# A two-layer trunk on one core: the first norm's order and c's row, the low parts of the out stage, and the place of the tiles in memory

## The chip, the core and the metric

The kernel runs on one core of one Trainium2 chip. The core has five engines that run side by side, each with its own instruction stream: TensorE (PE in the profile; its weight loads are listed as PEld), VectorE (DVE), ScalarE (ACT), GpSimd (POOL) and SyncE (SP), which issues most of the DMA transfers. Engines wait for one another by semaphores. Operands lie in SBUF (128 partitions), matmul results in PSUM.

The metric is the device time of one execution in microseconds. The time of a kernel is the median of its runs. Times inside the kernel come from one execution that the hardware profiler recorded.

## What is computed

A trunk of two layers over 512 frames of 1024 channels, in fp32. Cut to what matters here (first the silu of the conditioning vector c, from which each layer's six rows of shift, scale and gate come):

```python
def rms_norm(x, g):
    return x * lax.rsqrt(jnp.mean(x * x, axis=-1, keepdims=True) + 1e-6) * g

c_act = jax.nn.silu(c)                               # c: 1024 values
for l in range(2):
    sh1, sc1, gt1, sh2, sc2, gt2 = jnp.split(c_act @ ada_w[l] + ada_b[l], 6)
    h = rms_norm(x, norm1_g[l]) * (1 + sc1) + sh1
    p = h @ w_in[l]                                  # and v_down for the second layer
    ...                                              # token shift, split of p
    y_a = rwkv7_time_mix(...)                        # chunks of 64 frames, 8 heads
    y_b = multiscale_pool(...)
    mixed = br_gate[0] * (y_a @ proj_a[l]) + br_gate[1] * (y_b @ proj_b[l])
    x = x + gt1 * (mixed @ w_out[l])
    h2 = rms_norm(x, norm2_g[l]) * (1 + sc2) + sh2
    gate, up = jnp.split(h2 @ w_gu[l], 2, axis=-1)
    x = x + gt2 * ((silu(gate) * up) @ w_down[l])
return rms_norm(x, final_g)
```

## The kernel before

x is kept with channels on the partitions: eight tiles of 128 channels x 512 frames. A norm therefore needs sums over partitions, which TensorE makes.

**Products in three parts.** For accuracy every fp32 operand of the large products is split into a high part (rounded to the type fp32r) and a low part (what is left). A `block` is three matmuls: high weights by high data, high weights by low data, low weights by high data (`hh,whi`, `hl,whi`, `hh,wlo`). All matmuls go through one helper, so all of them have line L221. `weights` (from L179) makes the two parts of a weight tile of 128x1024 that SP has fetched (`raw`): ScalarE casts the high part (L195), and the low part is made in one of two ways. Either VectorE subtracts (L201), or, while `self.by_dma` is set, ScalarE writes the negative of the raw tile (L198) and GpSimd issues a DMA that adds the weight from memory once more onto it, the rounding being left over since the destination was written as fp32r (L199):

```python
if self.by_dma and (self.by_dma is True or self.count % self.by_dma):
    nc.scalar.activation(lo, raw, AF.Copy, scale=-1.0)
    nc.gpsimd.dma_start(lo, src, accum_op=ALU.add)
else:
    self.on(nc.vector, "tensor_tensor")(lo, raw, hi.bitcast(F32), ALU.subtract)
```

Of the tiles that the profile names, `hh` and `hl` are the parts of the normed x, `yah` and `yal` those of the time-mixing result, `mh` and `ml` those of the merged branches (`mixed`), `f`, `fh`, `fl` those of the channel mixer's inner values, `th`, `tl`, `f13h`, `f13l` those of products of 256 columns in the mixer (function `seven`), in which seven products take the place of eight.

**The head** (`head`, from L294) is the first norm. SP issues c, given out to all 128 partitions in the transfer (L299), the eight pieces of x (L302), two tables of constants (L304, L305), the first two rows of ada_w (`raw`, L255) and then pieces of w_in (`wr`, L322). ScalarE takes the Silu of c on all partitions (`cact`, L310) and the squares of the pieces of x (`ssum` for the first, `sq` for the others, L398 and L401; two buffers), VectorE sums the squares (L402). In `rstd` TensorE then multiplies the sum with a column of 1/1024 (`m<-mean,ssum`), ScalarE takes the root (`r`, L413), VectorE the reciprocal (L414), and multiplies it into four diagonal matrices (`dg`, L417); one product of them with ones (`m<-dg,ones`) gives the factor of each frame on all partitions. VectorE then makes `nt` (x times that factor, L354), ScalarE `nh` (scale and shift, L356), and w_in's first products, in plain fp32 (`acc<-nh,wr`), begin. The shift and scale (`mods`) come from VectorE's passes over rows of ada_w times cact (`modulation`, L264, two instructions each, a custom operation and a read-out), and `gsc` (L289) joins the scale with the norm's gain. `soon` (L391) is a tiny activation that loads a function table of ScalarE ahead of its use.

**The order of the work.** A scheduler orders each engine's instructions by the dependencies and the order in which the code issues them. Where the code sets `pinned` (for TensorE) or `exact` (for ScalarE and VectorE; `on` consults it), the order of the program is kept.

**The out stage** stands at the end of the mixer of each layer, behind the last chunks of the time mixing. `side` (L512) multiplies the pooled branch with proj_b and the gate (`hh`, `hl` in L533 are its results here, kept in buffers of those names). `mixer` (from L1131) then loops over eight output tiles m: twelve matmuls of proj_a with `yah`, `yal`; the gate `g` comes by DMA, `g` times the product (L1150), plus the other branch (L1151), then the split into `mh` on ScalarE (L245) and `ml` on VectorE (L246). In the loop the weights of proj_a (four tiles) and the first two of w_out are prepared. `by_dma` is set in the stages before and is switched off behind this loop, ahead of the products with w_out. `yn` (L1010) and `yal` (L1029) belong to the last step of the time mixing.

**Memory.** Tiles are laid out in pools that are opened and closed from both ends of SBUF. By the tables of the built program the places of the tiles within 512 bytes are: whi, wlo, hh, hl and raw at 96; f, fh, fl, th, tl, f13h, f13l and the other factors at 480; xi, wr, mh, ml at 160; two small pools at 64. No matmul operand of the three-part products lies at 0.

Of the kernel before, what the change touches and what calls it, by code (L numbers as in the profile page):

```python
# [17 lines left out]
DRAM = bass.MemoryType.DRAM  # L18

P = 128  # L20
D = 1024
S = 512
L = 2
# [50 lines left out]
FINAL = (6, 3)  # L74

WHOLE = 3

EARLY = ((2, 5, 5, 4), (3, 6, 6, 6))

# [42 lines left out]
class Trunk:  # L122
    def __init__(self, ctx, tc, a, out):
        self.ctx, self.tc, self.nc, self.a, self.out = ctx, tc, tc.nc, a, out
        self.pinned, self.last, self.by_dma = False, None, False
        self.third, self.turn, self.ahead, self.on_way, self.land = None, 0, 1, [], []
        self.count, self.fetched = 0, []
        self.hf, self.exact, self.later, self.keep = None, False, [], 0
        self.after = None
        nc = self.nc  # L130
        pool = lambda **k: ctx.enter_context(self.pool(**k))
        self.const = pool(name="const", bufs=1)
        self.wraw = pool(name="wraw", bufs=3)
        self.whl = pool(name="whl", bufs=2)
        self.hp = pool(name="hp", bufs=1)
        self.psum = pool(name="psum", bufs=4, space=PSUM)
        self.dram = pool(name="dram", bufs=1, space=DRAM)
        self.cst = self.const.tile([P, N_CST], F32, name="cst")
        self.cols = self.const.tile([P, N_COLS], F32, name="cols")
        self.ones = self.const.tile([P, P], F32, name="ones")  # L140
        self.mean = self.const.tile([P, 1], F32, name="mean")
        self.eps = self.const.tile([P, 2], F32, name="eps")
        self.mods = [self.const.tile([P, 48], F32, name=f"mods{l}") for l in range(L)]
        self.gsc = [self.const.tile([P, 16], F32, name=f"gsc{l}") for l in range(L)]
        self.omm = [self.const.tile([P, 15], F32, name=f"omm{l}") for l in range(L)]
        self.omka = [self.const.tile([P, 4], F32, name=f"omka{l}") for l in range(L)]
        self.xs = [self.dram.tile([P, S], F32, name=f"xs{k}") for k in range(KC)]
        self.yb = {
            (n, g): self.dram.tile([P, S], F32, name=f"{n}{g}") for n in ("yh", "yl") for g in range(4)
        }  # L150
        self.vf = [self.dram.tile([P, S], F32, name=f"vf{j}") for j in range(NJ)]
        self.hd = {k: self.dram.tile([P, S], F32, name=f"hd{k}") for k in AWAY}
# [141 lines left out]
    def head(self, w0):  # L294
# [1 line left out]

        nc, a = self.nc, self.a
        self.cact = self.const.tile([P, D], F32, name="cact")
        nc.sync.dma_start(self.cact, a["c"].partition_broadcast(P))  # L299
        xin = [w0.tile([P, S], F32, name=f"xi{k}", bufs=1) for k in range(KC)]  # L300
        for k in range(KC):
            nc.sync.dma_start(xin[k], a["x"][k])  # L302
        at = CST["block"][0]
        nc.sync.dma_start(self.cst[:, 0:at], a["cst"][:, 0:at])  # L304
        nc.sync.dma_start(self.cols, a["cols"])  # L305
        nc.gpsimd.memset(self.ones, 1.0)
        nc.gpsimd.memset(self.mean, 1.0 / D)
        nc.gpsimd.memset(self.eps[:, 0:1], EPS_RMS)
        nc.gpsimd.memset(self.eps[:, 1:2], EPS_GN)
        nc.scalar.activation(self.cact, self.cact, AF.Silu)  # L310
        raws, ws = {}, []

        def rows(k):
            for i in (KC + k, k):
                raws[i] = self.rows(0, i, w0)

        raw = [w0.tile([P, D], F32, name=f"wr{i}", bufs=1) for i in range(KRV0)]
        cut = WHOLE * P
        rows(0)
        for i in range(KRV0):  # L320
            if i != GV:
                nc.sync.dma_start(raw[i][:, 0:cut], a["w_in"][0, i][:, 0:cut])  # L322
# [2 lines left out]
        for i in range(KRV0):  # L325
            at = 0 if i == GV else cut
            nc.sync.dma_start(raw[i][:, at:], a["w_in"][0, i][:, at:])
        for k in range(KC):
            self.square(xin[k], k, ALL)
        self.soon(AF.Sqrt)  # L330
        self.new_h()
        rb = self.rstd(ALL)
        self.soon(AF.Sigmoid)
        nh = []
        banks = self.banked(raw)
# [12 lines left out]
        for k in range(KC):  # L348
            if k >= WHOLE:
                rows(k)  # L350
            self.modulation(0, (KC + k, k), raws)
            self.gains(0, 0, k, k + 1)
            t = self.tmp.tile([P, S], F32, tag="nt", name="nt", bufs=2)
            nc.vector.tensor_tensor(t, xin[k], rb, ALU.mult)  # L354
# [49 lines left out]
    def rstd(self, hs, between=lambda: None):  # L404
# [4 lines left out]
        for w in range(n):  # L409
            at = hs.start + w * P  # L410
            self.mm(st[:, w : w + 1], self.ssum[:, at : at + P], self.mean, start=True, stop=True)
        r = self.tmp.tile([P, 4], F32, tag="r4", name="r4", bufs=2)
        nc.scalar.activation(r[:, 0:n], st[:, 0:n], AF.Sqrt, bias=self.eps[:, 0:1])  # L413
        nc.vector.reciprocal(r[:, 0:n], r[:, 0:n])  # L414
        dg = self.tmp.tile([P, S], F32, tag="sq", name="dg", bufs=2)
        for w in range(n):
            nc.vector.tensor_scalar(  # L417
                dg[:, w * P : (w + 1) * P], self.c("ident"), r[:, w : w + 1], None, ALU.mult
            )
        between()  # L420
        rb = st[:, 0 : n * P]
        self.mm(rb, self.ones, dg[:, 0 : n * P], start=True, stop=True)
# [2 lines left out]
    def turned(self, hs, g):  # L425
# [1 line left out]
        nc = self.nc  # L427
        n, half = (hs.stop - hs.start) // P, KC // 2
        st = self.m()
        r = self.tmp.tile([P, 4], F32, tag="r4", name="r4", bufs=2)  # L430
# [600 lines left out]
    def mixer(self, l):  # L1031
# [35 lines left out]
        with ExitStack() as ctx:  # L1067
# [53 lines left out]
            with self.pool(name="ch", bufs=1) as sc:  # L1121
                for step in self.chain(l, sc):
                    self.go(gates, CHAIN[step])
            self.pinned = False
            proj = [self.weights(self.a["proj_a"][l, 0])]
            self.go(gates)
        ya = [(self.ya[0][:, j, :], self.ya[1][:, j, :]) for j in range(NJ)]
# [539 lines left out]
```

## Time and profile before

| | |
|---|---|
| runs | 1476.82 us median, 1475.88 to 1486.47, 3 runs |
| profiled execution, its own time | 1479.65 us |
| its span in the trace | 1477.9 us |
| granted TensorE clock over the span | 0.995 |
| instructions recorded | 25375 |
| DMA | 299.28 MB, mean 203 GB/s |
| POOL busy | 246.8 us (17%) x291 |
| low parts by ScalarE and DMA (L198) | 65, mean 1053 ns |

The page divides the span into 40 slices; in nearly all of them TensorE is busy nine tenths or more, in the first five tenths and in the seventh and the last eight:

```profile
PE   5999998999999999999999999999999999999998
...
DVE  7888958576788888876767685768578888887333
...
PEclk9999999999999999999999999999999999999999
```

A digit is the busy share of a slice in tenths, in the row PEclk the granted clock. A row of the groups (as for L201 in the prediction) gives line, engine, operation, result and operands, shapes and count; then busy time and the mean of one in ns; then the idle time of the engine just before and what ended it. Matmuls overlap, since a next one starts before the last has drained: the duration of one (0.39 us for 512 columns) is longer than the distance to the next start (about 0.23), and the distance is what it costs.

The share of the busy time is an average over all stages. A wait of TensorE costs time where TensorE has nothing else to do; a wait of another engine costs nothing as long as TensorE is not kept by it.

### The profile page before, as it was taken

The page shows a single profiled execution, that of the slowest core. Times are in us where ns is not written, and L with a number is a line of the kernel's source. Part 1 is how long each engine was busy: PE and PEld are TensorE (multiplying, and loading weights), DVE is VectorE, ACT ScalarE, POOL GpSimd, SP SyncE. Part 2 cuts the span into 40 slices and gives each one's busy share as a digit, 9 for nine tenths or more (in the row PEclk, how much of TensorE's full clock was granted, in tenths as well). Part 3 has the DMA queues.
Part 4 walks back from the last instruction along what each step waited for, and adds up shares of the span by engine and source line. Part 5 has one row for each costly group of instructions (what it writes and reads, how often), then busy time and mean ns, then how long its engine had stood idle before and what let it go on. Part 6 is the DMA issues. An engine that isn't in the chain of part 4 may idle for free. (4 is left out here: it accounts for less than half of the span.)

```text
span 1477.9 us, 25375 instructions
## 1 busy us (share of the span) xinstructions
PE 1429.7 (97%) x9982; PEld 1219.6 (83%) x9982; DVE 1087.3 (74%) x1846; ACT 751.0 (51%) x1031; POOL 246.8 (17%) x291
## 2 busy tenths in 40 slices
PE   5999998999999999999999999999999999999998
PEld 2767676777899999988897777877789999998887
DVE  7888958576788888876767685768578888887333
ACT  5576544344456656642336766443444656656221
POOL 0133321110022211100012334111102222110000
PEclk9999999999999999999999999999999999999999
DMA  8788689589839999778726747976974899885232
GB/s 319 235 268 238 193 227 254 148 261 271 236 101 230 234 215 226 179 251 287 260 87 180 181 113 168 261 176 191 289 235 131 208 219 223 192 187 169 87 100 71
DMA packets 112918, 299.28 MB, mean 203 GB/s; under 512 B 12128, under 2 KB 22624, under 8 KB 112800
## 3 DMA queue, kind: packets, MB, share of 16 engines
q1 hardware_dynamic: 90160, 227.93, 47.3%
q0 software_dynamic: 21776, 68.69, 25.5%
q8 instruction: 78, 1.28, 0.4%
q10 hardware_dynamic: 864, 1.05, 0.2%
q14 instruction: 40, 0.33, 0.1%
HBM read 269.84 MB, written 27.79 MB: 201 GB/s over the span
## 5 line engine op out<-in xcount | busy, mean ns | idle before, releaser
L221 PE MATMUL acc<-hh,whi 128*128 128x512 f32 (+1 forms) x1119 | 392.5, 357 | 0.2
L221 PE MATMUL acc<-hh,wlo 128*128 128x512 f32 (+1 forms) x1111 | 379.2, 346 | 8.3 <-DMA wlo<-in_w_in 7.5
L221 PE MATMUL acc<-hl,whi 128*128 128x512 f32 (+2 forms) x1119 | 369.3, 346 | 0.1
L195 ACT CAST whi<-raw 128x1024 fp32r<-128x1024 f32 x143 | 149.8, 1049 | 266.8 <-PE acc L221 175.2
L221 PEld LDWEIGHTS acc<-hh,wlo 128*128 128x128 f32 x1111 | 210.7, 190 | 36.7 <-DMA wlo<-in_w_in 9.2
L221 PEld LDWEIGHTS acc<-hh,whi 128*128 128x128 f32 x1119 | 212.1, 190 | 31.9 <-issue 2.4
L221 PEld LDWEIGHTS acc<-hl,whi 128*128 128x128 f32 (+1 forms) x1119 | 203.8, 189 | 26.4 <-issue 2.2
L201 DVE TENSOR_TENSOR wlo<-raw,whi 128x1024 fp32r<-128x1024 f32 x78 | 94.7, 1221 | 77.3 <-ACT whi L195 72.9
L221 PE MATMUL acc<-f,whi 128*128 128x512 f32 (+1 forms) x304 | 92.2, 386 | 0.0
L221 PE MATMUL m<-tl,f13h 128*128 128x256 f32 x304 | 86.0, 283 | 0.0
L221 PE MATMUL m<-th,f13l 128*128 128x256 f32 x304 | 86.0, 283 | 0.0
L221 PE MATMUL m<-th,f13h 128*128 128x256 f32 x304 | 85.9, 283 | 0.0
L241 ACT CAST f24h<-x 128x1024 fp32r<-128x1024 f32 x38 | 39.9, 1050 | 60.4 <-DVE x L241 60.4
L198 ACT ACTIVATE wlo<-raw 128x1024 fp32r<-128x1024 f32 x65 | 68.5, 1053 | 0.1
L221 PEld LDWEIGHTS acc<-f,whi 128*128 128x128 f32 x304 | 56.2, 188 | 12.3
L199 POOL DMA_DIRECT2D wlo<-in_w_in x41 | 35.9, 876 | 159.3 <-ACT wlo L198 159.3
L1283 POOL DMA_DIRECT2D f22l<-in_w_gu x38 | 32.8, 863 | 171.6 <-ACT f22l L241 164.4
L221 PE MATMUL acc<-f,wlo 128*128 128x512 f32 (+1 forms) x152 | 58.7, 386 | 0.0
L241 DVE TENSOR_TENSOR f24l<-x,f24h 128x1024 fp32r<-128x1024 f32 x38 | 46.5, 1224 | 16.3 <-ACT f24h L241 16.3
L221 PEld LDWEIGHTS m<-th,f13h 128*128 128x128 f32 x304 | 58.4, 192 | 0.0
L221 PEld LDWEIGHTS m<-th,f13l 128*128 128x128 f32 x304 | 58.4, 192 | 0.0
L221 PEld LDWEIGHTS m<-tl,f13h 128*128 128x128 f32 x304 | 58.2, 192 | 0.0
(338 smaller groups left out, 3434.0 us busy)
## 6 DMA issues: line engine op xcount, KB each, us to landing
raw<-in_w_in SPq DMA_DIRECT2D x63, 512.0 KB, 4.7
raw<-in_w_gu SPq DMA_DIRECT2D x50, 512.0 KB, 4.5
raw<-in_w_down SPq DMA_DIRECT2D x44, 512.0 KB, 3.5
wlo<-in_w_in POOLq DMA_DIRECT2D x41, 512.0 KB, 7.7
wlo<-in_w_gu POOLq DMA_DIRECT2D x40, 512.0 KB, 6.8
x<-in_w_gu SPq DMA_DIRECT2D x76, 256.0 KB, 4.4
row<-in_ada SPq DMA_DIRECT2D x30, 512.0 KB, 5.2
raw<-in_ada SPq DMA_DIRECT2D x25, 512.0 KB, 4.9
```

The source lines that it names most:

```text
L195: self.on(nc.scalar, "copy")(hi, raw)
L198: nc.scalar.activation(lo, raw, AF.Copy, scale=-1.0)
L199: nc.gpsimd.dma_start(lo, src, accum_op=ALU.add)
L201: self.on(nc.vector, "tensor_tensor")(lo, raw, hi.bitcast(F32), ALU.subtract)
L221: i = (tensor.transpose if transpose else tensor.matmul)(*args, **k).ins
L241: return (lambda *a, **k: self.tc.keep_in_program_order(op(*a, **k))) if self.exact else op
L1283: nc.gpsimd.dma_start(lo, two[:, b], accum_op=ALU.add)
```

## The change

Three things are changed.

**The first norm.** x goes ahead of c in SP's queue. c comes as one row of 1024 values on one partition, behind the second piece of x, and the tables behind the fourth. TensorE gives c out to all partitions by two products with a row of ones (`spread`), and ScalarE takes the Silu of each half (`cact`) from PSUM, between the squares of x. The squares have four buffers. Twelve products of 128x128 ones with themselves, whose results nobody reads, stand in front on TensorE, 14 behind c's products, five between the mean and the product with the diagonals and five behind that (`WARM`). The four diagonals of this norm are made alternately on VectorE and ScalarE. TensorE's order is pinned here, and ScalarE's and VectorE's is that of the program. The modulation by row 0 of ada_w stands behind the norm's factor in the program, that by row 8 ahead of it.

**The out stage.** `by_dma` is switched off one loop earlier, behind the last chunks and ahead of the first weight of proj_a, so that six weights per layer get their low part by VectorE's subtraction.

**The layout.** Two unused tiles, of 88 and of 120 values per partition, shift the other tiles, so that by the tables of the built program nearly all operands of the three-part products lie at multiples of 512 bytes (the exceptions are tiles of two small pools at 96). The small tile r4 moves to the pool of constants.

```diff
+PADS = (88, 120)
...
+WARM = (12, 14, 5)
...
+        self.const.tile([P, PADS[0]], F32, name="pad")
+        pool(name="edge", bufs=1, side="right").tile([P, PADS[1]], F32, name="edge")
...
         self.cact = self.const.tile([P, D], F32, name="cact")
-        nc.sync.dma_start(self.cact, a["c"].partition_broadcast(P))
         xin = [w0.tile([P, S], F32, name=f"xi{k}", bufs=1) for k in range(KC)]
+        c = w0.tile([1, D], F32, name="c", bufs=1)
...
+        at = CST["block"][0]
         for k in range(KC):
             nc.sync.dma_start(xin[k], a["x"][k])
-        at = CST["block"][0]
-        nc.sync.dma_start(self.cst[:, 0:at], a["cst"][:, 0:at])
-        nc.sync.dma_start(self.cols, a["cols"])
+            if k == 1:
+                nc.sync.dma_start(c, a["c"].rearrange("(p n) -> p n", p=1))
+            if k == 3:
+                nc.sync.dma_start(self.cst[:, 0:at], a["cst"][:, 0:at])
+                nc.sync.dma_start(self.cols, a["cols"])
+        rows(0)
...
-        nc.scalar.activation(self.cact, self.cact, AF.Silu)
...
+        self.soon(AF.Silu)
+        self.pinned = True
+        ps = [self.m() for _ in range(3)]
+        idle = lambda n: [self.mm(ps[2][:, 0:P], self.ones, self.ones, start=True, stop=True) for _ in range(n)]
+        idle(WARM[0])
+
+        def spread(i):
+            cs = slice(i * S, i * S + S)
+            self.mm(ps[i], self.ones[0:1, :], c[:, cs], start=True, stop=True)
+            nc.scalar.activation(self.cact[:, cs], ps[i], AF.Silu)
...
+        self.ssum = w0.tile([P, S], F32, name="ssum", bufs=1)
         for k in range(KC):
-            self.square(xin[k], k, ALL)
+            sq = w0.tile([P, S], F32, tag="sq", name="sq", bufs=4) if k else self.ssum
+            nc.scalar.activation(sq, xin[k], AF.Square)
+            if k:
+                nc.vector.tensor_tensor(self.ssum, self.ssum, sq, ALU.add)
+            if k in (4, 5):
+                spread(k - 4)
+        idle(WARM[1])
         self.soon(AF.Sqrt)
+        self.exact = True
+        self.modulation(0, (KC,), raws)
         self.new_h()
-        rb = self.rstd(ALL)
+        rb = self.rstd(ALL, lambda: idle(WARM[2]))
+        idle(WARM[2])
+        self.modulation(0, (0,), raws)
+        self.exact = self.pinned = False
...
         dg = self.tmp.tile([P, S], F32, tag="sq", name="dg", bufs=2)
         for w in range(n):
-            nc.vector.tensor_scalar(
-                dg[:, w * P : (w + 1) * P], self.c("ident"), r[:, w : w + 1], None, ALU.mult
-            )
+            o = dg[:, w * P : (w + 1) * P]
+            if n == 4 and w % 2:
+                self.on(nc.scalar, "activation")(o, self.c("ident"), AF.Copy, scale=r[:, w : w + 1])
+            else:
+                self.on(nc.vector, "tensor_scalar")(o, self.c("ident"), r[:, w : w + 1], None, ALU.mult)
...
             self.pinned = False
+            self.by_dma = False
             proj = [self.weights(self.a["proj_a"][l, 0])]
```

The instructions that this leaves on an engine stand as follows. First TensorE at the start of the kernel, before (result, operands, size; `x4` is four in a row):

```order
L221 MATMUL m<-mean,ssum 128x1 x4
L221 MATMUL m<-dg,ones 128x512
L221 MATMUL acc<-nh,wr_147 128x512
L221 MATMUL acc<-nh,wr_148 128x512
L221 MATMUL acc<-nh,wr_150 128x512
```

and the same start after the change:

```order
L227 MATMUL m<-ones 128x128 x12
L227 MATMUL m<-c,ones 128x512 x2
L227 MATMUL m<-ones 128x128 x14
L227 MATMUL m<-mean,ssum 128x1 x4
L227 MATMUL m<-ones 128x128 x5
L227 MATMUL m<-dg,ones 128x512
L227 MATMUL m<-ones 128x128 x5
L227 MATMUL acc<-nh,wr_173 128x512
```

The products of ones and the two of c (`m<-c,ones`) are new; the order of the others is as it was.

Second, VectorE in the out stage of the first layer, from the last step of the time mixing into the loop over output tiles, before:

```order
L533 TENSOR_TENSOR hl<-acc,g 128x512
L1026 TENSOR_TENSOR b<-b,g 128x512
L533 TENSOR_TENSOR hh<-acc,g 128x512
L1029 TENSOR_TENSOR yal<-b,yah 128x4x128
L533 TENSOR_TENSOR hl<-acc,g 128x512
L1150 TENSOR_TENSOR g_3207<-acc,g_3207 128x512
L1151 TENSOR_TENSOR g_3207<-g_3207,hh 128x512
L246 TENSOR_TENSOR ml_3212<-g_3207,mh_3211 128x512
L1150 TENSOR_TENSOR g_3228<-acc,g_3228 128x512
L1151 TENSOR_TENSOR g_3228<-g_3228,hl 128x512
L246 TENSOR_TENSOR ml_3233<-g_3228,mh_3232 128x512
```

and after, where L207 is the subtraction of `weights`, L567 the old L533, L1060 and L1063 the old L1026 and L1029:

```order
L207 TENSOR_TENSOR wlo<-raw,whi 128x1024
L1060 TENSOR_TENSOR b<-b,g 128x512
L567 TENSOR_TENSOR hh<-acc,g 128x512
L1063 TENSOR_TENSOR yal<-b,yah 128x4x128
L567 TENSOR_TENSOR hl<-acc,g 128x512
L207 TENSOR_TENSOR wlo<-raw,whi 128x1024
```

Further on in the loop, after the change (L1185, L1186 and L252 are the old L1150, L1151 and L246):

```order
L1185 TENSOR_TENSOR g_3323<-acc,g_3323 128x512
L207 TENSOR_TENSOR wlo<-raw,whi 128x1024
L1186 TENSOR_TENSOR g_3323<-g_3323,hl 128x512
L1185 TENSOR_TENSOR g_3344<-acc,g_3344 128x512
L252 TENSOR_TENSOR ml_3328<-g_3323,mh_3327 128x512
L1186 TENSOR_TENSOR g_3344<-g_3344,hh 128x512
L252 TENSOR_TENSOR ml_3349<-g_3344,mh_3348 128x512
```

Three subtractions stand ahead of the loop's first product and three within it, and from the fifth tile on the multiplication of the next tile stands ahead of the subtraction `ml` of the last one.

More of the change, by code (lines that the diff above doesn't have):

```diff
@@ L298, in head, with rows @@
         self.cact = self.const.tile([P, D], F32, name="cact")
-        nc.sync.dma_start(self.cact, a["c"].partition_broadcast(P))
         xin = [w0.tile([P, S], F32, name=f"xi{k}", bufs=1) for k in range(KC)]
+        c = w0.tile([1, D], F32, name="c", bufs=1)
+        raws, ws = {}, []
+        def rows(k, which=(KC, 0)):
+            for i in which:
+                raws[i + k] = self.rows(0, i + k, w0)
+        at = CST["block"][0]
         for k in range(KC):
             nc.sync.dma_start(xin[k], a["x"][k])
-        at = CST["block"][0]
-        nc.sync.dma_start(self.cst[:, 0:at], a["cst"][:, 0:at])
-        nc.sync.dma_start(self.cols, a["cols"])
+            if k == 1:
[4 more added lines that the diff above has]
+        rows(0)
         nc.gpsimd.memset(self.ones, 1.0)
@@ L309, in head @@
         nc.gpsimd.memset(self.eps[:, 1:2], EPS_GN)
[L310 to L315, printed above, removed]
+        self.soon(AF.Silu)
[7 more added lines that the diff above has]
+            nc.scalar.activation(self.cact[:, cs], ps[i], AF.Silu)
         raw = [w0.tile([P, D], F32, name=f"wr{i}", bufs=1) for i in range(KRV0)]
         cut = WHOLE * P
-        rows(0)
         for i in range(KRV0):
@@ L350, in head @@
                 rows(k)
-            self.modulation(0, (KC + k, k), raws)
+            if k:
+                self.modulation(0, (KC + k, k), raws)
             self.gains(0, 0, k, k + 1)
@@ L411, in rstd @@
             self.mm(st[:, w : w + 1], self.ssum[:, at : at + P], self.mean, start=True, stop=True)
-        r = self.tmp.tile([P, 4], F32, tag="r4", name="r4", bufs=2)
+        r = self.const.tile([P, 4], F32, tag="r4", name="r4", bufs=2)
         nc.scalar.activation(r[:, 0:n], st[:, 0:n], AF.Sqrt, bias=self.eps[:, 0:1])
-        nc.vector.reciprocal(r[:, 0:n], r[:, 0:n])
+        self.on(nc.vector, "reciprocal")(r[:, 0:n], r[:, 0:n])
         dg = self.tmp.tile([P, S], F32, tag="sq", name="dg", bufs=2)
         for w in range(n):
-            nc.vector.tensor_scalar(
-                dg[:, w * P : (w + 1) * P], self.c("ident"), r[:, w : w + 1], None, ALU.mult
-            )
+            o = dg[:, w * P : (w + 1) * P]
[3 more added lines that the diff above has]
+                self.on(nc.vector, "tensor_scalar")(o, self.c("ident"), r[:, w : w + 1], None, ALU.mult)
         between()
@@ L429, in turned @@
         st = self.m()
-        r = self.tmp.tile([P, 4], F32, tag="r4", name="r4", bufs=2)
+        r = self.const.tile([P, 4], F32, tag="r4", name="r4", bufs=2)
         out = self.hb[1].tile([P, n, D], F32, tag="hf1", name="y", bufs=1)
```

## Prediction

> **What bounds the kernel now.** I read the page's busy times first, then TensorE's waits, then the start of the timeline, and last the distance between the starts of neighbouring matmuls.
>
> ```profile
> PE 1429.7 (97%) x9982; PEld 1219.6 (83%) x9982; DVE 1087.3 (74%) x1846; ACT 751.0 (51%) x1031; POOL 246.8 (17%) x291
> ```
>
> TensorE (PE) works 97% of the span; 48 us are left in which it does not. So there are two ways to a gain: take away some of these 48 us, or make the matmuls themselves come closer together. TensorE's waits say where the 48 us lie:
>
> ```profile
> PE m L221 <- POOL omka L383: 13.2, 1, 13.2
> PE acc L221 <- DMA wlo<-in_w_in: 7.5, 4, 3.1
> ...
> PE acc L221 <- DMA wlo<-in_proj_a: 1.0, 1, 1.0
> PE acc L221 <- DVE yal L1029: 0.9, 1, 0.9
> ...
> PE acc L221 <- DMA wlo<-in_w_out: 0.5, 1, 0.5
> ...
> PE acc L221 <- ACT mh L245: 0.4, 1, 0.4
> PE acc L221 <- DVE ml L246: 0.2, 1, 0.2
> ```
>
> The columns are total, count and longest. The 7.5 us of w_in's low parts are in a stage that the change leaves alone. The 13.2 us are put down to a small GpSimd instruction that was long done; what TensorE really waits for at 13.17 is the last sum of squares, as the head's timeline shows (start, duration, engine, line):
>
> ```profile
> 0.75 0.39 SPq L299 DMA_DIRECT2D cact<-in_c  x1
> ...
> 5.43 1.06 ACT L310 ACTIVATE cact<-cact 128x1024 f32<-128x1024 f32 x1 [3.40 <-DMA cact<-in_c]
> ...
> 6.39 0.61 ACT L398 ACTIVATE ssum<-xi 128x512 f32<-128x512 f32 x1
> ...
> 7.55 5.47 DVE L402 TENSOR_TENSOR ssum<-ssum,sq 128x512 f32<-128x512 f32 x7 [7.55 <-ACT sq L401]
> ...
> 9.08 0.63 ACT L401 ACTIVATE sq<-xi 128x512 f32<-128x512 f32 x1 [0.17 <-DVE ssum L402]
> ...
> 13.17 1.84 PE L221 MATMUL m<-mean,ssum 128*128 128x1 f32 x8 [13.17 <-POOL omka L383]
> ...
> 15.05 0.27 ACT L413 ACTIVATE r<-m,eps 128x4 f32<-128x4 f32 x1 [1.43 <-PE m L221]
> ...
> 15.56 0.88 DVE L417 TENSOR_SCALAR dg<-cst,r 128x128 f32<-128x128 f32 x4
> ...
> 16.35 1.28 DVE L264 CUSTOM_DVE_ANT_0 raw<-raw,cact,cols 128x1024 f32<-128x1024 f32 x1
> ...
> 16.58 2.04 PE L221 MATMUL m<-dg,ones 128*128 128x512 f32 x2 [1.57 <-DVE dg L417]
> ...
> 18.66 1.28 DVE L354 TENSOR_TENSOR nt<-xi,m 128x512 f32<-128x512 f32 x2 [1.03 <-PE m L221]
> ...
> 20.25 4.60 PE L221 MATMUL acc<-nh,wr 128*128 128x512 f32 x6 [1.63 <-ACT nh L356]
> ...
> 24.69 2.74 PE L221 MATMUL m<-nh,wr 128*128 128x512 f32 x6
> ...
> 20.00:24.30 4.30, 4.05 (x6) 1.73 (x7) 4.03 (x8) 0.90 (x3) 0.00 (x0) 1.00 1.02 394
> ...
> 20.00:37.00 17.00, 16.75 (x35) 7.40 (x36) 16.37 (x27) 7.87 (x13) 0.06 (x2) 1.00 0.76 299
> ```
>
> Up to 20.25 us the head is one chain: x arrives, squares, their sum, mean, root, diagonals, a product that spreads them, nt, nh, first product. The last two rows are windows: length, busy time of PE, PEld, DVE, ACT, POOL, granted clock, DMA share, GB/s. From 20 to 37 us VectorE works 16.37 of 17 us, so that it sets the pace there; its work is the same after, so what nt gains the whole stretch gains.
>
> **The head.** *Transfers.* c's broadcast (128 x 4 KB = 512 KB) goes from the front of the queue, and a 4 KB row, 64 KB and 119 KB of constants come in before the last x. At the 394 GB/s of the full stretch from 20 us on the removal gives 1.33 us (524 thousand bytes) and the additions take 0.49; a piece of x takes 0.67. x0 lands 0.67 us ahead of c's present 5.43, at 4.76, and x7 at 4.76 + 7 x 0.67 + 0.49 = 9.9. *Squares.* Before, seven sums take 5.47 us, 0.78 each, since with two buffers every square waits 0.17 for VectorE. With four it does not; the sums cost 0.69 each (as the 128x512 operations below). ScalarE has eight squares of 0.63 and two Silus of 512, 0.61 each as its pass at 6.39: 6.3 us from 4.76, to 11.1. The last sum ends between 11.5 and 13.0 (no gain, were c's row late, since the Silu stands before the sixth square); I take 12.2, **-0.8**. *Clock.* TensorE's fp32 passes take 4.60/6 = 0.77 us at 20.25 and 2.74/6 = 0.46 at 24.69: about four us of unbroken work bring the full rate. A cold fp32 product of 512 columns is two such records, 1.53; one of 128 columns a quarter, 0.39; so the 12 idle products run from about 1 to 5.7 us, just when c's row is there, its two products to 7.6 or 8.8, and 14 more to 11 or 14. If that holds the clock up, the 1.84 and the 2.04 us halve: -0.9 and -1.0. *Diagonals* on two engines: 0.88 becomes about 0.5, -0.35. Together nt could start 3.1 us earlier, at 15.55. But VectorE's pass for row 0 (1.28 at 16.35, now hidden behind the 2.04) stands between the diagonals and nt: last sum 12.2, mean product with its hand-over to 13.25, root 0.27 and the 0.24 from its end to the diagonals' start to 13.8, diagonals to 14.35, the pass with read-out and gain 1.5, and nt at 15.85. **nt: 18.66 to 15.85, -2.8 us**. Ends: -0.5 (the clock not up, so that the idle products run past the last sum) to -4 (the sum at 11.5, VectorE's pass hidden). The idle matmuls between the diagonals and the product (five, at 0.23 with the full rate) lie within the 1.2 us in which root, reciprocal and diagonals are made; cold, at 0.39, they would cost 0.8 of the gain. GpSimd's and SP's queues lose nothing here: SP issues raw rows 8 and 0 directly behind x.
>
> The Trainium skill ("TensorE: Matmul & The Clock Gate", Part 1: The HAM clock gate) says that the clock is throttled by default and released by roughly one window of 3.4 us of activity, and returns when a window is idle. By its window five us of idle products suffice, and the gap before the mean product would not close the gate; the traced step between 20.25 and 24.69 agrees with it.
>
> **The out stage.** Six weights per layer (proj_a 4, w_out 2) lose their ScalarE pass (L198) and accumulating DMA, and get one VectorE subtraction each.
>
> ```profile
> 1057.71 0.87 POOL L199 DMA_DIRECT2D wlo<-in_proj_a  x1 [6.57 <-ACT wlo L198]
> ...
> 1066.21 0.50 PE L221 MATMUL acc<-yah,wlo 128*128 128x512 f32 x1 [1.02 <-DMA wlo<-in_proj_a]
> ...
> 332.42 0.69 DVE L533 TENSOR_TENSOR hh<-acc,g 128x512 f32<-128x512 f32 x1 [3.13 <-PE acc L221]
> ...
> 338.70 0.69 DVE L246 TENSOR_TENSOR ml<-g,mh 128x512 fp32r<-128x512 f32 x1 [0.69 <-ACT mh L245]
> ...
> L201 DVE TENSOR_TENSOR wlo<-raw,whi 128x1024 fp32r<-128x1024 f32 x78 | 94.7, 1221 | 77.3 <-ACT whi L195 72.9
> ```
>
> In the second layer a low part is issued at 1057.71 and TensorE starts on it at 1066.21, having waited 1.02: the detour costs 8.5 us where the subtraction costs 1.22 behind the same cast. What goes: wlo of proj_a 1.0, of w_out 0.5, and with the loop written in a pipelined order mh 0.4 and ml 0.2, **-2.1 us**. What is added: 6 x 1.22 = 7.3 us of VectorE per layer. Its cover are VectorE's idle times: 3.13 us before hh, and 0.69 per output tile waiting for mh. In the loop a tile takes four times 0.69 with that wait, 2.72 us; without it 2.07, so eight tiles and three subtractions take 16.6 + 3.7 = 20.2 of 22 us. That fits with little to spare. Ends: -3.0 (yal's 0.9 goes too) to +0.9 (two subtractions exposed, 2.4, less 1.5). The wait for yal stays, as two subtractions and hh stand ahead of it.
>
> **The layout.** Tile addresses move to multiples of 512 bytes. Of the rows only the distance between starts shows what a matmul costs.
>
> ```profile
> 1397.95 0.40 PE L221 MATMUL acc<-fh,whi 128*128 128x512 f32 x1
> ...
> 1400.75 0.39 PE L221 MATMUL acc<-hh,whi 128*128 128x512 f32 x1
> ...
> 1406.20 0.62 PE L221 MATMUL acc<-f,whi 128*128 128x512 f32 x2
> ...
> 459.80 0.28 PE L221 MATMUL acc<-hh,whi 128*128 128x256 f32 x1
> ...
> 460.16 0.28 PE L221 MATMUL m<-th,f13h 128*128 128x256 f32 x1
> ...
> 461.36 0.28 PE L221 MATMUL m<-tl,f13h 128*128 128x256 f32 x1
> ...
> 403.77 0.28 PE L221 MATMUL acc<-hh,wlo 128*128 128x256 f32 x1
> ...
> 404.57 0.39 PE L221 MATMUL acc<-hl,whi 128*128 128x256 f32 x2
> ```
>
> The 12 starts from 1397.95 to 1400.75 (moving tile fh at 480 within 512 bytes, weights at 96) lie 0.2333 apart, the 24 to 1406.20 (hh and weights both at 96) 0.2271. With 256 columns it is the other way: 3 steps of 0.1200 from 459.80 with hh and weights at 96, 10 of 0.1200 from 460.16 with both at 480, and 7 of 0.1143 with hh at 96 and weights at 160. So it is the difference of the two addresses that shows, some 6 ns either way. Over all undisturbed pairs of starts, grouped by that difference (starts from the trace, addresses from the build), the 1,441 unequal 512-wide ones cost 4.1 ns more than the equal (5.9 us), and the 1,594 unequal 256-wide ones 1.5 ns less (2.4 us). After, nearly all are equal: **-5.9 + 2.4 = -3.5 us**. Ends: 0 (the effect belongs to something else, such as which tile is read) to -9 (the 6.2 ns on all 1,441, nothing lost).
>
> **Sum.** -2.8 - 2.1 - 3.5 = -8.4 us on the profiled execution's 1479.65 (span 1477.9): 1471.25. The median of the runs, 1476.82, is 2.8 lower; from it 1468.4.
>
> **Rivals.**
> 1. *Muted.* The equal offsets bring nothing, or c's row comes late, the Silu holds the squares and the clock falls back before the mean product. With one of them: -8.4 + 3.5 = -4.9, 1471.9; with both, -0.8 in the head and -2.1 behind it: 1473.9. For it: the head's gain is four terms that all must hold. That the change misses its purpose entirely (0) lies here too.
> 2. *The fixed part of a matmul falls.* 512 columns cost 0.2271, 256 cost 0.1200: 0.418 ns a column, which leaves 13 ns fixed, 97 us over 7,500 matmuls. No tile of before lies at offset 0. If there the fixed part shrinks by the 5.7 ns between 0.1200 and 0.1143 on all of them, -43 us: 1426. Against it: equal offsets at 96 and at 480 cost the same 0.120, so the place itself has shown no effect.
> 3. *Equal offsets at 0 collide.* Place: the 256-wide products, which get 1.5 ns slower already by the reckoning above. Another step of 5.7 ns on 4,300 of them is +24.5: 1492.9. It ends on the slower side of before from +2.0 ns (8.4 us over 4,300).
>
> **Chances.** Forecast (1462 to 1471) 0.53; muted 0.25; the fixed part falls, wholly or in part, 0.16; collision 0.06. A change within 1% (14.8 us) is about what a measurement of this kernel cannot tell from none. Rival 2 (0.16) and the best end of the forecast (0.06; all three terms at their good ends, -16) are over 1% faster: 0.22; the worse two thirds of the collision are over 1% slower: 0.04; the rest, 0.74, is between. The range leaves out some 0.12 of rival 2 below and 0.06 above: 1452 (a sixth of those 97 us of fixed part gone, with the rest) to 1478 (the small end of the collision).
>
> **What would show it.** The head: nt near 15.9 instead of 18.66, mean product about 0.9 instead of 1.84, the spread 1.0 instead of 2.04, first product near 17.4; wrong, if the mean product is still 1.8 or ScalarE waits for c's products. The out stage: no wait for wlo of proj_a or w_out, VectorE's subtractions in its idle time; wrong, if TensorE waits for wlo L207 or for ml. The layout: 512-wide starts 0.227 apart with fh, f too, 256-wide 0.120 everywhere; wrong, if fh still has 0.233, or any fp32r distance falls below 0.22. The forecast is wrong as a whole if the three places agree and the time does not.

## The result: 12.5 us less, a ratio of 0.991

The changed kernel takes 1463.89 us (median of 6 runs, 1462.41 to 1466.88) against 1476.35 before (6 runs): a ratio of 0.991, 95% interval 0.9883 to 0.9937 (the two medians alone give 0.9916). The forecast was 1468.4, 8.4 us less, its range 1452 to 1478. The sign and the range held. The three terms of which the sum was made did not: one was a fourth of what it should be, and the experiments leave open whether the three add.

The profiled execution took 1464.27 us (span 1462.5). Its page, first row: TensorE is busy for 4.9 us more than before, since the idle products count as work, and the span is 15.4 us shorter.

```profile
PE 1434.6 (98%) x10058; PEld 1235.8 (84%) x10058; DVE 1098.6 (75%) x1856; ACT 740.4 (51%) x1023; POOL 235.5 (16%) x279
```

The head of the changed kernel, in the timeline (start, duration, engine, line):

```profile
1.00 4.87 PE L227 MATMUL m<-ones 128*128 128x128 f32 x24 [1.00 <-POOL mean L323]
...
3.47 0.63 ACT L350 ACTIVATE ssum<-xi 128x512 f32<-128x512 f32 x1 [1.22 <-DMA xi<-in_x]
...
6.26 0.63 ACT L350 ACTIVATE sq<-xi 128x512 f32<-128x512 f32 x1 [1.57 <-DMA xi<-in_x]
...
10.79 1.49 DVE L352 TENSOR_TENSOR ssum<-ssum,sq 128x512 f32<-128x512 f32 x2 [0.17 <-ACT sq L350]
...
12.56 0.95 PE L227 MATMUL m<-mean,ssum 128*128 128x1 f32 x8
...
14.06 0.69 ACT L247 ACTIVATE dg<-cst,r 128x128 f32<-128x128 f32 x2 [0.24 <-DVE r L247]
...
14.46 1.28 DVE L247 CUSTOM_DVE_ANT_0 raw<-raw,cact,cols 128x1024 f32<-128x1024 f32 x1
...
14.81 1.13 PE L227 MATMUL m<-dg,ones 128*128 128x512 f32 x2
...
15.97 1.28 DVE L386 TENSOR_TENSOR nt<-xi,m 128x512 f32<-128x512 f32 x2 [0.22 <-PE m L227]
...
17.56 2.84 PE L227 MATMUL acc<-nh,wr 128*128 128x512 f32 x6 [0.51 <-ACT nh L388]
```

The last sum ends at 12.28, the mean product takes 0.95 instead of 1.84, the spread 1.13 instead of 2.04, nt starts at 15.97 instead of 18.66 and the first product at 17.56 instead of 20.25; its six records take 2.84, not 4.60.

The granted clock of this stretch, by windows (length, busy time of PE, PEld, DVE, ACT, POOL, granted clock, DMA share, GB/s):

```profile
5.10:8.40 3.30, 3.30 (x17) 1.93 (x17) 1.30 (x3) 2.07 (x4) 0.79 (x4) 1.00 1.03 354
8.50:11.80 3.30, 3.30 (x18) 3.30 (x17) 2.59 (x5) 2.89 (x6) 0.35 (x1) 0.50 1.03 410
12.00:15.00 3.00, 2.93 (x26) 2.74 (x25) 2.63 (x8) 2.04 (x6) 0.00 (x0) 1.00 1.06 392
```

The clock is full, falls to half between 8.5 and 11.8 us although TensorE is busy throughout, and is full again when the mean product starts at 12.56. Why it falls is not shown. Of the six other profiles with these idle products (e1, e5, e6, e8, e10, e12) all but e5 show the same dip. Where TensorE has only just begun to work the column is no guide: it reads 1.00 for the kernel before from 20.00 to 24.30 us too (in the prediction), where the products take the time of half rate; there the durations tell.

The out stage is best read from TensorE's waits in two windows. Before, from 320 to 410 and from 1040 to 1180 us (total, count, longest):

```profile
PE m L221 <- DVE ssum L402: 1.2, 1, 1.2
PE acc L221 <- DVE yn L1010: 1.1, 1, 1.1
PE acc L221 <- DVE yal L1029: 0.9, 1, 0.9
...
PE acc L221 <- DVE yn L1010: 1.6, 1, 1.6
PE acc L221 <- DMA wlo<-in_proj_a: 1.0, 1, 1.0
PE acc L221 <- DMA wlo<-in_w_out: 0.5, 1, 0.5
PE acc L221 <- ACT mh L245: 0.4, 1, 0.4
PE acc L221 <- DMA wlo<-in_w_gu: 0.3, 1, 0.3
PE m L221 <- DVE ssum L402: 0.3, 1, 0.3
PE acc L221 <- DVE ml L246: 0.2, 1, 0.2
```

These are 3.2 us in the first layer and 4.3 in the second. The changed kernel comes to the second of these stages some 9 us earlier, so its second window begins at 1020 us (before, TensorE has no wait between 1020 and 1040). One wait is left in each window, the one for yn:

```profile
PE acc L227 <- DVE yn L1044: 1.2, 1, 1.2
...
PE acc L227 <- DVE yn L1044: 1.1, 1, 1.1
```

So the wait for yn hardly changes, 2.3 us where it was 2.7. The others, 4.8 us together, are gone.

The layout shows in the distance between starts, here at the place that answers to the one of before (fh, then hh, in the last products of the second layer):

```profile
1383.79 0.39 PE L227 MATMUL acc<-fh,whi 128*128 128x512 f32 x1
...
1386.51 0.39 PE L227 MATMUL acc<-hh,whi 128*128 128x512 f32 x1
...
1391.95 0.62 PE L227 MATMUL acc<-f,whi 128*128 128x512 f32 x2
```

Twelve steps of fh take 2.72 us and 24 of hh 5.44: 0.2267 both, where fh had 0.2333. Over the whole trace the 512-wide fp32r matmuls without a stall behind them come to 8.0 us less than before, the 256-wide ones to 3.0 us more.

### The profile page after: what moved, and what is told of

It is laid out like the page before. It is cut to its first block, busy times and chain, and to the rows that moved or that the text cites. A ratio compares the mean times of both kernels' runs of the same rounds, so it can differ in the third digit from the quotient of the medians.

```text
span 1462.5 us, 25497 instructions
## 1 busy us (share of the span) xinstructions
PE 1434.6 (98%) x10058; PEld 1235.8 (84%) x10058; DVE 1098.6 (75%) x1856; ACT 740.4 (51%) x1023; POOL 235.5 (16%) x279
## 5 line engine op out<-in xcount | busy, mean ns | idle before, releaser
L207 DVE TENSOR_TENSOR wlo<-raw,whi 128x1024 fp32r<-128x1024 f32 x90 | 109.5, 1221 | 75.9 <-ACT whi L201 71.4
L247 ACT ACTIVATE s<-s 128x512 f32<-128x512 f32 x38 | 24.0, 632 | 64.7 <-DVE s L247 64.7
```

Source lines behind the costliest of these rows:

```text
L247: return (lambda *a, **k: self.tc.keep_in_program_order(op(*a, **k))) if self.exact else op
```

## The experiments

Every kernel was compared with the kernel before on the same chip, whose medians there were 1479.1 to 1479.7; microseconds less or more than before are the ratio's distance from 1 times these. First each part alone.

**The first norm's part, once with r4 in the pool of constants (e1) and once without (e10).** Edit of e1, against the changed kernel:

```diff
-        self.const.tile([P, PADS[0]], F32, name="pad")
-        pool(name="edge", bufs=1, side="right").tile([P, PADS[1]], F32, name="edge")
...
-            self.by_dma = False
             proj = [self.weights(self.a["proj_a"][l, 0])]
```

> Only the first norm's part of the change (x ahead of c, c by two products, four buffers of squares, idle products, diagonals on two engines); the low parts of the out stage stay with ScalarE and DMA, and the two unused tiles are left out, so that tile addresses stay unequal within 512 bytes (moving r4 shifts the left side by 64). Theory (three parts that add): 2.8 us less than before, the first product near 17.5 instead of 20.25, and nothing gained behind 90 us. Rival (what the head gains, the stages up to 320 us give back in their waits for transfers): 0 to 1.5 us less, with TensorE's waits for wlo of w_in and for sig longer by what was won.

Measured: 1476.39, ratio 0.9972 (0.9951 to 0.9992), some 4 us less. But the shift by r4 had changed the distances of its matmuls too (512-wide 2.5 us less in sum, 256-wide 1.0 less), so it tells nothing clean. In e10 r4 stands where it was, by this edit to e1, at both places where r4 is made:

```diff
-        r = self.const.tile([P, 4], F32, tag="r4", name="r4", bufs=2)
+        r = self.tmp.tile([P, 4], F32, tag="r4", name="r4", bufs=2)
```

> The first norm's part alone with r4 left where it was, so that all tile places are those of before. Theory (the 2.8 us at the start are mostly given back by 90 us, where VectorE sets the pace, and by the waits for transfers behind): 0 to 1.5 us less than before. Rival (they stay): 2.5 to 3 us less.

Measured: 1476.5, ratio 0.9988 (0.9971 to 1.0005): 1.8 us less, between the theory's range and the rival's. The interval, from 4.3 us less to 0.7 more, holds both, and no change too, so the run does not decide between them. Where r4 alone is moved (e11):

> Only r4 moved to the pool of constants, which shifts the left side by 64 bytes and turns differences of 384 and 128 into 320 and 192. Theory (from the probe, 512 columns cost 229.3 ns at 320 instead of 233.5, 686 times, and 256 columns 117.8 at 192 instead of 118.3, 1,121 times): 3.5 us less than before. Rival (what matmuls gain here is waited for elsewhere): within 1 us.

Measured: 1477.45, ratio 0.9982 (0.997 to 0.9994), 2.7 us less. The matmuls' distances fell by the 3.4 us that the probe (below) gives. It leans to the theory, with the rival's 1 us just inside the interval.

**The out stage's part alone (e2).**

```diff
             self.pinned = False
+            self.by_dma = False
             proj = [self.weights(self.a["proj_a"][l, 0])]
```

> Only the out stage's part: the six low parts per layer by VectorE. Theory: the waits of TensorE between 320 and 410 us and between 1060 and 1120 us for wlo, yal, mh, ml and in the stage behind them go, 4 to 6 us less than before in all; no wait for wlo of proj_a or w_out is left. Rival (the gain seen there in the changed kernel comes from the layout, which lets matmuls stand closer in these stages): 2.1 us or less.

Measured: 1470.99, ratio 0.9946 (0.9935 to 0.9958): 8.0 us less, more than the theory's upper end and four times the rival's. Its TensorE waits in the two windows (the second again from 1020 us) are one each:

```profile
PE acc L221 <- DVE yn L1010: 0.6, 1, 0.6
...
PE acc L221 <- DVE yn L1010: 1.8, 1, 1.8
```

Only the wait for yn stays, 2.4 us where it was 2.7. The wait for yal is gone with no help from the layout. So are those behind the stage, for ssum and for w_gu's low parts.

**The layout alone (e3).** The two tiles, with 104 and 120 values:

```diff
+PADS = (104, 120)
...
+        self.const.tile([P, PADS[0]], F32, name="pad")
+        pool(name="edge", bufs=1, side="right").tile([P, PADS[1]], F32, name="edge")
```

> Only the two unused tiles (104 and 120 values here, since r4 stays where it was): nine in ten operand pairs at equal places within 512 bytes, most at 0. Theory (equal places cost 0.2275 for 512 columns and 0.120 for 256): 5 us less than before; distances 0.2275 and 0.1199. Rival 1 (the place 0 itself matters, also to transfers and other engines): 7 us less or more. Rival 2 (no effect of its own): within 1.5 us.

Measured: 1477.2, ratio 0.9992 (0.9973 to 1.0011), 1.2 us less. For the time rival 2 is favoured: the theory's 5 us lie outside the interval, which reaches from 4.0 us less to 1.6 more. The distances were as the theory said (512-wide 6.6 us less in sum, 256-wide 1.8 more, 4.8 net), and the gain did not arrive at the end: in its profile the stalls are 5.1 us longer.

**The probe (e4)**: the cost of a distance by itself. In the first series the moving tile mv stays and the weights move by 32 bytes from wa to wb and on:

```diff
+        for n in (512, 256):
+            for d in STEPS:
+                ps = psum.tile([P, S], F32, tag="by", name="by")
+                for j in range(COUNT):
+                    at = j % 8 * P + d // 4
+                    self.mm(ps[:, 0:n], ws[d][:, at : at + P], mv[:, 0:n], start=j == 0, stop=j == COUNT - 1)
```

> No part of the trunk: 24 matmuls each of 512 and of 256 columns for sixteen differences between the place of the weights and that of the moving tile (steps of 32 bytes), then the same with both moved together; the output is not the reference's. Theory (the difference alone decides): with both moved together all sixteen cost the same, about 0.227 and 0.120; with a difference 512 columns cost up to 0.233 and 256 down to 0.114. Rival (it is the place of one operand, or which engine writes beside it): the two series show the same steps, or neither shows any.

The timeline, one row for each 24 matmuls. First 512 columns with the weights moved on by 0, 32, 192 and 256 bytes (wa, wb, wg, wi), then 256 columns by 0 and 96 (wa, wd), then mv moved along with the weights, by 64:

```profile
24.46 5.61 PE L135 MATMUL by<-mv,wa 128*128 128x512 f32 x24
29.91 5.75 PE L135 MATMUL by<-mv,wb 128*128 128x512 f32 x24
...
57.91 5.67 PE L135 MATMUL by<-mv,wg 128*128 128x512 f32 x24
...
69.02 5.61 PE L135 MATMUL by<-mv,wi 128*128 128x512 f32 x24
...
113.57 3.03 PE L135 MATMUL by<-mv,wa 128*128 128x256 f32 x24
...
122.11 2.98 PE L135 MATMUL by<-mv,wd 128*128 128x256 f32 x24
...
170.00 5.64 PE L135 MATMUL both<-mv,wc 128*128 128x512 f32 x24
```

Moved together, every place costs the same, 5.64 us, but for 5.66 in the first row of that series (place 0): no place is better than another, 0 included. With the weights moved alone, 512 columns cost 226.7 ns at 0 and at 256 bytes, 229.3 at 192 and 448, and 233 to 234 at all others; 256 columns cost 119.6 at 0 and 256, 120.1 at 160 and 416, and 117.3 to 118.4 at all others. So the difference within 256 bytes sets these steps. It is not everything: in the series moved together 512 columns cost 227.8 ns (228.6 in its first row, whose operands are those of the first row of all at 226.7), and what makes this up to 1.9 ns is not shown. The theory holds, but for the size at 256 columns, where the 0.114 of the prediction came from seven steps and the means do not fall below 117.3.

**One thing altered in the changed kernel.** It was run once more beside three others (e5).

> The changed kernel once more, beside the three that each alter one thing in it, so that they are compared on one chip. 12 to 13 us less than before (the first measurement gave a ratio of 0.991).

Measured: 1463.8, ratio 0.9891 (0.9869 to 0.9913). Without the two tiles (e6; r4 stays in the pool of constants):

```diff
-        self.const.tile([P, PADS[0]], F32, name="pad")
-        pool(name="edge", bufs=1, side="right").tile([P, PADS[1]], F32, name="edge")
```

> The changed kernel without the two unused tiles: 1,200 matmuls of 512 columns and 1,230 of 256 have operands at different places within 256 bytes again. Theory (faster matmuls pay where TensorE sets the pace; with the low parts by DMA the layout's gain went into longer waits, with VectorE's it stays): 4 to 5 us slower than the changed kernel beside it. Rival (the layout is worth the 1.2 us that it gave alone, the rest lies in waits for transfers that do not care when TensorE asks): 0 to 1.5 us slower.

Measured: 1461.23, ratio 0.9875 (0.9853 to 0.9897). Not slower at all, if anything 2.6 us faster, with intervals that overlap. I had overlooked that r4's move alone gives most of the distances' gain: against e5 the 512-wide matmuls lose 5.1 us and the 256-wide win 3.9, 1.2 net. The theory's price was wrong by that, and the time does not show even the 1.2: the stages below tell why. Without the idle products (e7):

```diff
-WARM = (12, 14, 5)
+WARM = (0, 0, 0)
```

> The changed kernel without the idle products of ones (their results are read by nobody). Theory (they hold the clock up): the mean product takes 1.8 us again and the spread 2.0, nt starts near 17.8 instead of 16.0, the first products of w_in run at half rate up to about 22 us; 2 us slower than the changed kernel. Rival (VectorE sets the pace from 20 to 37 us, and TensorE waits there for hh and hl anyway): nt later as in the theory, but of what the first products lose nothing is seen behind 40 us.

Measured: 1466.2, ratio 0.9909 (0.9889 to 0.9928), 2.4 us slower than e5, intervals overlapping. The profile agrees with the theory up to the first products (start, duration):

```profile
12.34 1.84 PE L227 MATMUL m<-mean,ssum 128*128 128x1 f32 x8 [4.41 <-DVE ssum L352]
...
15.47 2.08 PE L227 MATMUL m<-dg,ones 128*128 128x512 f32 x2 [1.29 <-ACT dg L247]
...
17.58 1.28 DVE L386 TENSOR_TENSOR nt<-xi,m 128x512 f32<-128x512 f32 x2 [1.17 <-PE m L227]
...
19.17 5.41 PE L227 MATMUL acc<-nh,wr 128*128 128x512 f32 x6 [1.62 <-ACT nh L388]
```

After the twentieth record of real work e7 is 3.3 us behind e5, after the 250th (86 us) 0.6: the rival is right that little of it survives. The kernel that came early then waits: in e5 TensorE waits 1.3 us for hh and 0.4 for hl, two waits that e7 does not have. The Trainium skill ("TensorE: Matmul & The Clock Gate", Part 1: The HAM clock gate) has the clock throttled until a window of activity releases it; the 0.95 against 1.84 for the same eight records, with and without the products of ones ahead, agree.

With the mixer's sums 96 bytes aside (e8):

```diff
             t = next(sums)
+            tp.tile([P, 24], F32, name="skew")
```

> The changed kernel with 96 unused bytes behind the tiles th and tl of the mixer's sums, which moves these to 416 within 512 bytes while all other operands stay at 0: 1,368 matmuls of 256 columns have a difference of 416. Theory (from the probe, 117.3 ns at this difference against 119.6): 3 us less than the changed kernel, 3.1 from 1,368 times 2.3 ns. Rival (VectorE and DMA behind it set the pace in that stage, or the step is not seen when other engines read beside): within 1 us.

Measured: 1462.19, ratio 0.9876 (0.9854 to 0.9899). The 1,368 distances fell to 117.5 ns and the sum of the 256-wide by 3.8 us against e5; of that 1.6 us are seen in the medians, which cannot be told from none. The stages tell it better: the products lie in the two channel stages, and these take 1.9 us less each (340.7 and 327.2 against 342.6 and 329.1 in the table below). So the theory holds there, in full size, and the rival does not.

**The out stage taken back (e12)**, the head and the layout kept:

```diff
             self.pinned = False
-            self.by_dma = False
             proj = [self.weights(self.a["proj_a"][l, 0])]
```

> The changed kernel with the out stage's low parts by ScalarE and DMA again. Theory (that part alone gave 8.0 us and the parts add): 7 to 9 us slower than the changed kernel, about 1472 where the changed one has 1464. Rival (with the head and the layout the stage starts earlier or runs faster, so that its waits for DMA are longer): more than 10 us slower.

Measured: 1478.13, ratio 0.9993 (0.9978 to 1.0008): 12 to 15 us slower than the changed kernel by the two ratios of that (0.991 and 0.9891), and not to be told from the kernel before. The rival is favoured. In the window of the second layer TensorE now waits more for w_out's low parts, 2.1 us where it was 0.5, and mh 0.8 where it was 0.4:

```profile
PE acc L227 <- DMA wlo<-in_w_out: 2.1, 2, 1.4
...
PE acc L227 <- ACT mh L251: 0.8, 1, 0.8
```

The time that TensorE needs from one and the same instruction to another tells it stage by stage (in us, one profile each, so that a single run's scatter is in it; the boundaries lie at 88.8, 311.9, 417.1, 761.4, 1024.0 and 1141.0 us of the kernel before):

```
                       start  mixing  out+norm  channel  mixing  out+norm  channel
                              layer 0 layer 0   layer 0  layer 1 layer 1   layer 1
before                  88.8   223.1   105.2     344.3    262.6   117.0     330.7
e2  out                 88.3   221.8   101.2     343.6    262.6   113.0     330.2
e10 head                84.9   218.5   106.4     343.5    262.3   118.0     330.6
e3  layout              88.9   221.8   106.2     342.5    264.0   118.5     329.1
e11 r4                  88.4   219.7   105.8     341.9    265.5   119.8     328.5
e12 head+layout         85.4   218.9   106.2     342.6    261.3   119.4     329.2
changed                 86.0   222.1   101.4     342.6    262.8   112.5     329.2
changed, again (e5)     86.4   220.7   101.8     342.6    264.4   112.3     329.1
e6  without tiles       85.9   220.9   102.0     341.9    261.7   112.5     328.5
e8  sums aside          86.8   222.8   101.5     340.7    262.7   112.5     327.2
```

With the low parts by DMA the two out stages take 105 to 106 and 117 to 120 us, whatever else is done; with VectorE's they take 101 to 102 and 112 to 113. This is the largest step in the table, and it repeats. With the low parts by DMA they are longer than before whenever something else is changed, but not the more the earlier TensorE comes: e3 reaches the first one 1.2 us early and e12 7.6 us, and both take 106.2.

The channel stages repeat far better, and there the distances arrive whole. The two together take 673.8 to 675.0 us where the places are those of before (before, e2, e10), 670.4 with r4 moved alone (e11, e6), 671.6 to 671.8 with the two tiles (e3, e12, the changed kernel), and 667.9 in e8. The 3.8 us of e8 are just what its distances lost. And the two tiles cost these stages 1.3 us: against e6 the 512-wide matmuls win 2.6 us there and the many 256-wide ones lose 3.8. The mixing stages vary by up to 5 us from one profile to the next, which hides what the tiles win in them.

**The traffic (e9).** Edit, against e2, in `weights` (it applies to the same six weights per layer):

```diff
             self.on(nc.vector, "tensor_tensor")(lo, raw, hi.bitcast(F32), ALU.subtract)
+            if self.spare is not None:
+                nc.gpsimd.dma_start(self.spare.tile([P, 1024], F32, tag="spare", name="spare"), src)
```

> The out stage's part alone (as in the earlier run of it), with GpSimd copying the same six weights per layer from memory to an unused place in memory behind each subtraction, so that the transfers stay and nobody waits for them. Theory (the low parts came late: the pass, the issue and the landing stood between the cast and the product): 7 to 8 us less than before, as without the copies. Rival (the traffic of the accumulating transfers held up the gates, the pieces of x and the next stage's weights): half of the 8 us or more is lost again, and TensorE waits for sums of squares or wlo of w_gu behind the stage.

Measured: 1486.05, ratio 1.0038 (1.002 to 1.0057), 14 us slower than e2. But it does not answer the question: since the copies depend on nothing, the scheduler put all twelve at the start of GpSimd's queue, as the timeline shows.

```profile
1.38 2.16 POOL L203 DMA_DIRECT2D spare<-in_proj_a  x4 [0.33 <-issue]
...
26.30 0.96 POOL L203 DMA_DIRECT2D spare<-in_w_out  x2
```

In its out stages (101.3 and 112.7 us) there was no such traffic. Its start took 104.2 us instead of 88.3: 6.3 MB more in the head cost 15.9 us.

## Why the forecast held, and where its terms did not

**The head: right in its sizes up to nt, in part by luck.** The last sum was forecast at 12.2 and ended at 12.28; mean product 0.92 and 0.95; nt 15.85 and 15.97; the gain at nt 2.8 and 2.7. But the way there was another. The first square started at 3.47 and not at 4.76, and ScalarE then waited 1.57 us for the next pieces of x, a wait that the text did not have; the two errors nearly cancel. VectorE's pass for row 0 did not stand in nt's way: it ended at 15.74, and nt waited 0.22 more for the product of the diagonals, which started at 14.81 since ScalarE's two diagonals (0.69 us, forecast at about 0.5) ended only then. And the idle products did not hold the clock up without a break; it came back in time for the mean product. That "what nt gains the whole stretch gains" held to 86 us (2.4 and 2.8 in the changed kernel's two profiles). Alone the head was worth 1.8 us, with an interval that holds 2.8 and none.

**The out stage: right in direction, wrong in size by a factor of four.** The term was -2.1, and the part alone gave -8.0. The step that failed is the list of "what goes". It took the waits that name a low part or a part of mh, and left out ssum (1.5 us), yal (0.9) and w_gu's low parts (0.3). With the 0.3 us that yn lost, 5.1 us of waits went in e2. Its two out stages are 8.0 us shorter in the table; the other 2.9 us are not in that view.

For yal the text said that it stays "as two subtractions and hh stand ahead of it". They do stand ahead, but VectorE was not short of time there. Before, it idled 3.13 us ahead of hh at 332.42. The row puts this down to TensorE, whose product for this tile was done at 329.9. What came last was the gate g of this tile, a DMA transfer: by the trace's semaphores it landed at 332.33, 6.8 us after its issue. In e2 it landed at 328.14, 4.5 us after its issue, and yal was in time. The issues, before and in e2, and then hh and yal in e2:

```profile
325.50 0.33 SPq L525 DMA_DIRECT2D g<-gd  x1
...
323.68 0.33 SPq L525 DMA_DIRECT2D g<-gd  x1
...
328.38 0.69 DVE L533 TENSOR_TENSOR hh<-acc,g 128x512 f32<-128x512 f32 x1
329.15 0.69 DVE L1029 TENSOR_TENSOR yal<-b,yah 128x512 fp32r<-128x512 f32 x1
```

The subtractions' cover held: no wait for wlo L207, and none for ml.

So the accumulating transfers were not only late themselves, they went together with later gates. From 320 to 365 us of the kernel before and of e2 (busy share of the DMA engines in 40 slices, tenths; then KB each and the median from issue to landing):

```profile
DMA  9999999999999999999999999999979879999940
...
g<-gd SPq DMA_DIRECT2D x8, 256.0 KB, 6.3
...
x<-in_x SPq DMA_DIRECT2D x5, 256.0 KB, 11.4
```

```profile
DMA  9999999999917607049575866575648941797879
...
g<-gd SPq DMA_DIRECT2D x7, 256.0 KB, 3.0
x<-in_x SPq DMA_DIRECT2D x5, 256.0 KB, 4.5
```

Before, the engines are full for nearly all of the window; in e2 they are full for the first 11 slices and then have gaps, and gates and x land in less than half the time. How much of the 8 us is that and how much the shorter way of the low parts was to be told by e9, which does not answer it. For yal the gate's landing shows that it was the transfers; for the rest it stays open.

**The layout: the distances right, most of the term not in the time.** Equal places do make 512 columns cheaper and 256 dearer, as the row pairs had it, and the sum over the trace came to -5.0 instead of -3.5. But alone it gave 1.2 us (interval -4 to +1.6), and without the two tiles the changed kernel was no slower. What failed is the step from a shorter distance to a shorter time. It holds in the channel stages, to 0.1 us in e8, but more than half of what the places win lies in other stages, where it is not seen. And the two tiles are no help to it: moving r4 alone makes the channel stages shorter than r4 and the tiles together.

**The sum: near, in part by luck, and not shown to add.** The out stage was 5.9 us better than its term, the layout 2.3 and the head 1.0 worse, each measured alone; the errors have opposite signs. The three parts alone give 1.8, 8.0 and 1.2 us, 11.0 together, where the whole change gave 13.3 and 16.1 by its two ratios. The head and the layout together are worth 1.0 us with the old out stage (e12) and 5 to 8 with the new one (ratios of 0.991 and 0.9891 against 0.9946 in e2). That speaks for parts that help each other, but the intervals of the single runs are several us wide and it is not shown. Nor do the stages show where e12 loses: its out stages are 1.0 and 2.4 us longer than before, yet its profile, which is the fastest of its runs (1471.63 to 1485.31, median 1478.13), is 8 us faster than the profile of before. Where the time goes in its other runs, the profiles do not show.

**The rivals.** Of the muted case, the layout alone did bring almost nothing in the time; c's row came in time (TensorE took it at 5.80), and the clock was up when the mean product came. The out stage outweighed what was missing. Rival 2 and rival 3 are refuted by the probe: no place costs less or more than another. The change of 0.9% came out near the border of 1% on which the chances were set.

No version is shown to beat the changed kernel in its time: e6 and e8 are 2.6 and 1.6 us lower, with intervals that overlap its own. Their channel stages are faster by 1.3 and 3.8 us, so both are worth more runs.

## What to carry to other kernels

A wait that names one tile is a poor price for a stage whose transfers are full: look at the DMA engines' busy share in that window first, and count all waits of the stage and of the one behind it as candidates. Where a row names an engine that had long been done, look for the transfer that landed last. Runs of the whole kernel scatter by more than most parts are worth, so measure a part in the stage where it acts, by the time from one instruction to another, and use the stages that repeat. A window in us moves with the kernel: shift it when stages come earlier. In an experiment that adds work, tie the work to its place by a dependency, or the scheduler moves it.

## What the runs showed of the hardware

In the probe a matmul of 512 fp32r columns takes 226.7 ns from start to start if its moving operand and its weights lie at the same place within 256 bytes (227.8 to 228.6 in a second series), 229.3 if the moving operand lies 64 bytes further on, and 233 to 234 otherwise; with 256 columns it is 119.6 at the same place, 120.1 with the weights 160 bytes further on, and 117.3 to 118.4 otherwise. The place itself does not matter. Products of ones ahead halve the time of the mean product that follows (0.95 us against 1.84), though the granted clock fell to 0.50 for a while (8.5 to 11.8 us) with TensorE busy. What they win is soon waited for elsewhere: 3.3 us at 21 us of the kernel, 0.6 at 86. A 256 KB transfer landed 6.3 us after its issue (median) while the DMA engines were full, and 3.0 where they had gaps.
